# A two-layer decoder step on one core: the second layer's weight loads issued by GpSimd instead of SyncE

## The chip, the core and the metric

The kernel runs on one core of a Trainium2 chip. The core has a matrix engine (TensorE, "PE" in the profile, with its weight loads as "PEld"), a vector engine (VectorE, "DVE"), an activation engine (ScalarE, "ACT"), a general engine (GpSimd, "POOL") and SyncE ("SP"), which does no arithmetic and issues most of the transfers. Each engine takes its instructions strictly in order. A transfer is issued by one engine and carried out by the core's 16 DMA engines. The metric is the device time of one execution in microseconds (us). Lower is better.

## The reference, cut to what matters

One inference step of a two-layer hybrid decoder, for a prompt of 2048 positions and 8 short sample sequences:

```
layer 0:  u = rmsnorm(x); q, k, v, gate, g_low = split(u @ a_w_in)
          o = gated linear attention over chunks (4 heads)
          h = x + (rmsnorm(o) * silu(gate)) @ a_w_out
shared:   k, v = rope(rmsnorm(u @ w_k)), u @ w_v        # once, u = rmsnorm(h)
layer 1:  q, gate = split(rmsnorm(h) @ b_w_in)          # 2048 columns each
          o = attention of q over the last 128 positions and itself, with sinks, 32 heads on 4 key heads
          y = h + (o * silu(gate)) @ b_w_out
```

All is asked in float32. The kernel gets this from float16 products by splitting every factor into a high and a low half and taking three products (`PASSES`).

## The kernel before

The prompt is cut into 16 blocks of 128 positions (`NCH`). Three stages matter here.

**Layer 0 and the preparation.** While layer 0 runs, the weights of layer 1 are prepared beside it. `Unit.prepare` loads a raw float32 piece, scales and splits it (`convert`) and writes the halves to a DRAM tensor `pre`. These writes are issued by GpSimd (`pool.dma_start`, `pre<-pst` in the profile). `form_steps` does the same for the output weights: it forms seven combinations of quarter matrices (`wfd[0]` to `wfd[6]`, `wf<-...`), also written by GpSimd.

**Layer 1, the attention (from about 1420 us).** The loop `for t in range(-3, NKV * NCH)` runs over 64 (group, block) pairs: four groups `g` of 8 heads, 16 blocks in each. An iteration weaves the projections of block `t + 3` (24 matmuls for q, 24 for the gate, 24 more for keys and values in group 0), the scores of block `t + 1` (four steps "A") and the products with the values of block `t` (two steps "B"), by the string `ORDER`. The order of the matmuls is written out by hand (`pin`). For a block:
- `q_norm` squares q on ACT, sums on DVE, takes the power on POOL (`rs_m`, `rs_r`), multiplies on DVE (`KQ<-pj,rs_r`) and rotates on POOL (`KQ<-KQ,bt`, `S<-KQ,bt`, `KQ<-KQ,S`). `q_split` splits (`qe<-KQ`, ACT then DVE) and SyncE transposes by DMA (`X<-qe`, two buffers). `X` is the stationary operand of the scores (`o<-gl,X`, `lev<-gl,X`).
- `scores` takes the softmax numerators; each pair of heads ends in a DMA transpose on SyncE (`sth<-v` and `pst<-v`, two buffers each) that the value products need (`kv<-gl,sth`, `kv<-gl,pst`).
- `last` gates the result; `spill_halves` splits it on ACT and POOL (`ogT`), transposes (`og<-ogT`) and writes it out (`oge<-og`).

So SyncE issues six transposes per block besides the plain transfers.

The weights of a group are 8 units of 512 KB (4 of q, 4 of the gate; 4 more for the shared keys and values in group 0). `Unit.fetch` loads each with one DMA into the ring `W` of 12 buffers (`NW`). A group's fetches are put into the program when block 12 of the group before is reached (`run(gw[g + 1].steps())`); a fetch has to wait until PE has done with the buffer that it overwrites.

**The last stage (from about 2500 us).** y is computed for pairs of blocks with the seven prepared factors `wfd[n]`, seven products for a pair (`Pair`). `wform` loads a factor into four `W` buffers and `wform_big` into one buffer of the ring `uT` (four buffers, until then the normed activations), each in four quarters of 512 KB. They are put into the attention loop at fixed iterations (`n == TOT - 14`, `TOT - 7`, `TOT - 4`) and by a list `trickle` at its end.

Outside a few stretches (`fixed`), a planner that models the engines' times chooses the order of instructions on every engine but PE from the order of the program and from what is ready. `sync` and `pool` are thin wrappers around the engines' issue functions.

Of the kernel before, what the change touches and what calls it, by code (L numbers as in the profile page):

```python
# [75 lines left out]
def _body(tc, nc, cp, sb, ps, dr, i, o):  # L76
# [6 lines left out]
    def T(tag, shape, dt, bufs=None):  # L83
        return sb.tile(shape, dt, tag=tag, name=nm(tag), **({} if bufs is None else {"bufs": bufs}))
# [44 lines left out]
    dve, pool, sync = Queue(nc.vector), Queue(nc.gpsimd), Queue(nc.sync)  # L129
# [27 lines left out]
    wfd = [dr.tile([P, 8, 2, 512], F16, tag=f"wf{n}", name=f"wf{n}") for n in range(7)]  # L157
# [59 lines left out]
    class Unit:  # L217
# [62 lines left out]

        def fetch(self):
            self.t = T("W", [P, 2, 1024], F16, NW)
            sync.dma_start(self.t, self.pre)

        def __call__(self, k, hl, s):
            return self.t.rearrange("p z (k c) -> p z k c", c=self.ncol)[:, hl, k, s]
# [789 lines left out]
    pin[0] = True  # L1076
    us[0].load()
    fetch()
    us[1].load()
    fetch(2)  # L1080
    us[2].load()
    fetch()
    us[3].load()
    fetch(7)
# [689 lines left out]
    def wform_big(n, x, box={}):  # L1774

        if x == 0:
            t = box[n] = T("uT", [P, 8, 2, 512], F16, 4)
            wf[n] = lambda k, hl, s=ALL: t[:, k, hl, s]
        ks = slice(2 * x, 2 * x + 2)
        sync.dma_start(box[n][:, ks], wfd[n][:, ks])  # L1780

    def wform(n, x, ts={}):

        t = ts[n, x] = T("W", [P, 2, 2, 512], F16, NW)
        sync.dma_start(t, wfd[n][:, 2 * x : 2 * x + 2])
        wf[n] = lambda k, hl, s=ALL: ts[n, k // 2][:, k % 2, hl, s]

    quarters = lambda f, n: [lambda x=x: f(n, x) for x in range(4)]
# [147 lines left out]
    for t in range(-3, NKV * NCH):  # L1936
        fill = []
        n = t + 3
# [41 lines left out]
        if n in (TOT - 7, TOT - 4):  # L1980
            run(quarters(wform_big, {TOT - 7: 0, TOT - 4: 2}[n]))
        if n == TOT - 14:
            run(quarters(wform, 3))
        if n == TOT - 1:
            trickle += [lambda x=x: pairs[0].load(x) for x in (3, 2)] + quarters(wform_big, 1)
            summing += pairs[0].sums()
        if n == TOT:
            trickle += quarters(wform, 4) + quarters(wform, 5)
        if n == TOT + 1:
            trickle += quarters(wform_big, 6)  # L1990
# [5 lines left out]
    for p_ in range(NCH // 2):  # L1996
# [8 lines left out]
        if p_ in (3, 4):  # L2005
            n = p_ - 3
# [87 lines left out]
```

## Time and profile before

| | |
|---|---|
| runs | 2772.89, 2778.55, 2779.77 us; median 2778.55 |
| the profiled execution's own time | 2779.74 us |
| its span in the profile | 2778.0 us |
| busy in the span | PE 2705.4, DVE 1699.3, ACT 1388.3, POOL 1135.7 us |
| mean granted TensorE clock | 0.992 |
| bytes moved by DMA | 425.35 MB, of which 385.87 MB by the queue of SyncE (q1), 36.09 MB by GpSimd's (q0) |

The profile's times are measured from the start of the span. A line of a view of groups names the source line (nearly all are helpers' lines, L102 for matmuls and L123 for the rest, so the tiles tell what it is), the engine, the operation and the tiles as out<-in. "SPq" is SyncE issuing. The duration of an issue on SP holds its waits; on POOL it is the time that GpSimd is busy with it.

### The profile page before, as it was taken

The numbers are of one execution on the slowest core, as the hardware profiler recorded it, in microseconds if no ns is written. First come the engines' busy times: TensorE is split into PE (matmuls) and PEld (weight loads), VectorE is DVE, ScalarE is ACT, GpSimd is POOL, SyncE is SP. The second block draws the span as 40 slices with busy tenths as digits, with TensorE's granted clock in tenths as the row PEclk, the third lists the DMA queues.
The fourth block names the chain that finished last, engine by engine and source line by source line (L and its number), as shares of the span: only waits on it lengthen the run. The fifth ranks groups of instructions, "written<-read, shape, count | busy, mean of one in ns | idle before, by whom it ended". The sixth has DMA issues, their size and how long they took to land.

```text
span 2778.0 us, 52040 instructions
## 1 busy us (share of the span) xinstructions
PE 2705.4 (97%) x19378; PEld 1389.7 (50%) x19378; DVE 1699.3 (61%) x3476; ACT 1388.3 (50%) x3235; POOL 1135.7 (41%) x1600
## 2 busy tenths in 40 slices
PE   8999999999999999999999999999999999989999
PEld 5444444544454444445445555555555555544444
DVE  7565656666656664446314656677777777777653
ACT  7664645565556554433213555566666666541110
POOL 4334334333423331136206777576566567530000
PEclk9999999999999999999999999999999999999999
DMA  5543335343534345789766778978978889896431
GB/s 171 129 110 92 99 95 139 105 120 109 144 92 128 112 141 168 223 264 274 218 195 128 135 152 161 216 141 152 201 134 152 192 154 187 162 225 196 148 102 58
DMA packets 800135, 425.35 MB, mean 153 GB/s; under 512 B 636368, under 2 KB 708760, under 8 KB 799848
## 3 DMA queue, kind: packets, MB, share of 16 engines
q1 hardware_dynamic: 786632, 385.87, 59.0%
q0 software_dynamic: 11168, 36.09, 3.6%
q8 instruction: 151, 2.47, 0.4%
q14 instruction: 104, 0.85, 0.1%
q10 hardware_dynamic: 2080, 0.07, 0.0%
HBM read 178.75 MB, written 106.50 MB: 103 GB/s over the span
## 4 chain that ended last, share of the span: by engine, by line
PE 62%; DVE 10%; DMA 9%; ACT 9%; POOL 5%; issue 5%; SPq 0%; ACTq 0%; POOLq 0%; DVEq 0%
PE pj L102 35%; PE tr L102 11%; PE o L102 11%; PE kv L102 3%; DMA pst<-v 2%; ACT o L123 2%; PE lev L102 2%; DVE v L123 2%; POOL KQ L123 1%; ACT v L123 1%; DMA W<-in_state_gla_dram 1%; DVE W L123 1%; ACT L123 1%; DVE o L123 1%; DVE X L123 1%
## 5 line engine op out<-in xcount | busy, mean ns | idle before, releaser
L102 PE MATMUL pj<-W,uT 128*128 128x512 f16 x5088 | 1209.8, 382 | 5.5 <-DVE KQ L123 4.0
L102 PEld LDWEIGHTS <-uT 128*128 128x128 f16 x6976 | 651.0, 98 | 698.7 <-issue 24.5
L102 PE MATMUL tr<-W,uT 128*128 128x512 f16 x1536 | 365.6, 379 | 0.0
L123 POOL TENSOR_TENSOR KQ<-KQ,bt 128x256 f32<-128x256 f32 (+1 forms) x176 | 182.7, 1038 | 261.8 <-DVE X L123 207.8
L102 PEld LDWEIGHTS <-X 128*128 128x128 f16 x2744 | 185.0, 98 | 139.1 <-issue 11.1
L123 ACT ACTIVATE o<-o,mx 128x256 f32<-128x256 f32 (+1 forms) x384 | 168.6, 439 | 168.6 <-DVE mx L123 164.7
L123 POOL TENSOR_SCALAR rs_m<-ss 128x1 f32<-128x1 f32 (+3 forms) x186 | 41.8, 225 | 512.9 <-DVE ss L123 392.6
L123 DVE CUSTOM_DVE_ANT_0 o<-o,madd,nsink 128x256 f32<-128x256 f32 (+1 forms) x384 | 183.8, 479 | 45.4 <-PE o L102 41.1
L123 DVE SCALAR_TENSOR_TENSOR v<-o,v 128x512 f16<-128x512 f32 (+1 forms) x192 | 128.9, 672 | 102.7 <-ACT v L123 99.9
L123 POOL TENSOR_TENSOR rs_r<-rs_m,mhalf 128x1 f32<-128x1 f32 (+3 forms) x182 | 184.5, 1014 | 14.2
L102 PEld LDWEIGHTS <-W 128*128 128x128 f16 x2448 | 125.9, 97 | 86.3 <-issue 1.9
L102 PEld LDWEIGHTS <-v 128*128 128x128 f16 x976 | 95.1, 98 | 115.3 <-issue 2.3
L102 PEld LDWEIGHTS <-sg 128*128 128x128 f16 x800 | 77.6, 98 | 93.4 <-issue 1.2
L123 ACT ACTIVATE X<-KQ 128x512 f16<-128x512 f32 x128 | 84.6, 661 | 75.7 <-PE lev L102 42.6
L123 POOL TENSOR_TENSOR ogT<-og,ogT 128x512 f16<-128x512 f32 x64 | 79.2, 1238 | 102.6 <-ACT ogT L123 102.6
L102 PE MATMUL o<-gl,X 128*128 128x256 f16 (+1 forms) x768 | 114.8, 273 | 4.3 <-DMA X<-qe 2.7
L123 ACT ACTIVATE v<-o 128x512 f16<-128x512 f32 (+1 forms) x192 | 111.2, 579 | 3.5
L123 ACT ACTIVATE lev<-lev,mx 128x256 f32<-128x256 f32 (+1 forms) x128 | 56.5, 441 | 104.8 <-DVE mx L123 102.7
L123 DVE TENSOR_TENSOR X<-KQ,X 128x512 f16<-128x512 f32 x128 | 98.7, 771 | 16.6 <-ACT X L123 15.2
L123 POOL DMA_DIRECT2D pre<-pst x72 | 50.8, 708 | 139.8 <-DVE pst L123 136.5
L123 POOL TENSOR_TENSOR bt<-bt 128x256 f32<-128x256 f32 (+6 forms) x112 | 50.1, 447 | 136.1 <-ACT bt L123 129.2
L102 PE MATMUL pj<-W,v 128*128 128x512 f16 x448 | 103.7, 379 | 0.1
(441 smaller groups left out, 4891.0 us busy)
## 6 DMA issues: line engine op xcount, KB each, us to landing
pre<-pst POOLq DMA_DIRECT2D x72, 256.0 KB, 3.8
W<-pre SPq DMA_DIRECT2D x36, 512.0 KB
ogd<-ogk SPq DMA_DIRECT2D x64, 256.0 KB
wraw<-in_b_w_in_dram SPq DMA_DIRECT2D x64, 256.0 KB
oge<-og SPq DMA_DIRECT2D x64, 256.0 KB
wraw<-in_a_w_in_dram SPq DMA_DIRECT2D x52, 256.0 KB
wraw<-in_a_w_out_dram SPq DMA_DIRECT2D x32, 256.0 KB
X<-in_x_prompt_dram SPq DMA_DIRECT2D x32, 256.0 KB
```

Of the source, the lines that this page charges most:

```text
L102: return order(nc.tensor.matmul(*a, **k))
L123: x = f(*a, **k)
```

## The change

Three issue calls go from SyncE to GpSimd. Sources, destinations, sizes and places in the program stay as they are.

```diff
         def fetch(self):
             self.t = T("W", [P, 2, 1024], F16, NW)
-            sync.dma_start(self.t, self.pre)
+            pool.dma_start(self.t, self.pre)
...
     def wform_big(n, x, box={}):
         if x == 0:
             t = box[n] = T("uT", [P, 8, 2, 512], F16, 4)
             wf[n] = lambda k, hl, s=ALL: t[:, k, hl, s]
         ks = slice(2 * x, 2 * x + 2)
-        sync.dma_start(box[n][:, ks], wfd[n][:, ks])
+        pool.dma_start(box[n][:, ks], wfd[n][:, ks])
...
     def wform(n, x, ts={}):
         t = ts[n, x] = T("W", [P, 2, 2, 512], F16, NW)
-        sync.dma_start(t, wfd[n][:, 2 * x : 2 * x + 2])
+        pool.dma_start(t, wfd[n][:, 2 * x : 2 * x + 2])
         wf[n] = lambda k, hl, s=ALL: ts[n, k // 2][:, k % 2, hl, s]
```

These calls issue 36 loads `W<-pre`, 16 loads `uT<-wf` and 12 loads `W<-wf`, 64 in all, of 512 KB each.

## The prediction

> **What bounds the kernel now.** I read the page first, then the windows of the stages.
>
> ```profile
> PE 2705.4 (97%) x19378; PEld 1389.7 (50%) x19378; DVE 1699.3 (61%) x3476; ACT 1388.3 (50%) x3235; POOL 1135.7 (41%) x1600
> q1 hardware_dynamic: 786632, 385.87, 59.0%
> q0 software_dynamic: 11168, 36.09, 3.6%
> ```
>
> PE is busy for 97% of the span, so a change that leaves the matmuls alone can gain only where PE stands still or runs at a lower clock. The table of windows shows where: busy time (and instructions) of PE, PEld, DVE, ACT and POOL, then the granted clock, the busy share of the DMA engines (packets may overlap, so it can pass 1) and GB/s.
>
> ```profile
> 1420.00:1460.00 40.00, 40.00 (x187) 18.14 (x186) 6.39 (x12) 5.53 (x14) 4.98 (x10) 1.00 0.79 246
> 1460.00:1730.00 270.00, 270.00 (x2037) 144.68 (x2036) 157.28 (x405) 143.12 (x413) 191.87 (x272) 1.00 0.74 142
> 1730.00:1760.00 30.00, 25.95 (x224) 13.41 (x222) 12.97 (x34) 12.70 (x36) 16.07 (x22) 0.89 1.08 287
> 1760.00:1966.00 206.00, 205.00 (x1848) 117.46 (x1846) 153.21 (x404) 133.49 (x405) 132.63 (x164) 1.00 0.81 152
> 1966.00:1994.00 28.00, 25.30 (x252) 14.55 (x251) 20.94 (x51) 17.18 (x53) 16.32 (x24) 1.00 1.04 253
> 1994.00:2194.00 200.00, 199.32 (x1805) 114.19 (x1801) 148.33 (x393) 131.15 (x399) 131.26 (x163) 1.00 0.80 149
> 2194.00:2222.00 28.00, 24.89 (x225) 13.71 (x224) 19.15 (x47) 15.89 (x48) 15.38 (x22) 0.94 1.07 253
> 2325.00:2350.00 25.00, 22.65 (x191) 12.65 (x190) 18.09 (x48) 16.36 (x50) 15.37 (x21) 0.97 1.06 218
> 2386.00:2412.00 26.00, 23.18 (x199) 13.18 (x198) 17.41 (x44) 15.06 (x44) 14.58 (x19) 0.96 1.02 206
> 2436.00:2500.00 64.00, 52.21 (x495) 30.48 (x494) 45.63 (x100) 29.25 (x81) 16.67 (x21) 0.89 0.94 231
> ```
>
> The long quiet stretches lose almost nothing (1.0 us of 206, 0.7 of 200). All the loss of the attention stage sits in six short windows, and these are the windows with the moved loads: three changes of group (1730, 1966, 2194) and three places where factors are fetched (2325, 2386, 2436). There the DMA engines are at 0.94 to 1.08 against 0.80 between. PE's idle time there is 4.05 + 2.70 + 3.11 + 2.35 + 2.82 + 11.79 = 26.8 us. The clock takes more: the share not granted, times the window, is 3.3 + 1.7 + 0.75 + 1.0 + 7.0 = 13.8 us (0.11 of 30, 0.06 of 28, 0.03 of 25, 0.04 of 26, 0.11 of 64). So 40.6 us lie within reach, and hardly more. The view of PE's waits between 1420 and 2510 us (total, times, longest) says on what:
>
> ```profile
> PE kv L102 <- DMA pst<-v: 15.4, 6, 3.5
> PE pj L102 <- DVE KQ L123: 4.0, 1, 4.0
> PE lev L102 <- DVE v L123: 3.3, 1, 3.3
> PE o L102 <- DMA X<-qe: 2.7, 5, 0.7
> ```
>
> Mostly PE waits for transposes that SyncE issues; never for a weight load. One case in order of time, from the timeline:
>
> ```profile
> 2338.34 1.12 SPq L123 DMA_DIRECT2D uT<-wf  x2
> 2339.51 0.45 SPq L123 DMA_DIRECT2D bt<-rtd  x1
> 2340.07 1.78 SPq L123 DMA_TRANSPOSE pst<-v  x1
> 2347.70 0.47 PE L102 MATMUL kv<-gl,pst 128*128 128x64 f16 x10 [2.10 <-DMA pst<-v]
> ```
>
> The transpose stands right behind two 512 KB loads in the queue of SyncE; it is issued by 2341.85 and PE gets it only at 2347.70, 2.10 us late. The change of group at 1730 loses by another path with the same root:
>
> ```profile
> 1747.80 0.60 ACT L123 ACTIVATE E<-pj 128x512 f32<-128x512 f32 x1 [4.13 <-DMA out_cvp_dram<-E]
> 1752.52 1.03 PE L102 MATMUL pj<-W,uT 128*128 128x512 f16 x2 [4.05 <-DVE KQ L123]
> ```
>
> ACT waits 4.13 us for a small output transfer behind weight loads, and the norm after it (sum, POOL's power, `KQ`) holds PE for 4.05 us.
>
> **The change part by part.** It moves 64 issues: 36 `W<-pre`, 16 `uT<-wf`, 12 `W<-wf`. What they take now on SP, and what like transfers take on POOL (ns, smallest/median/largest; then landing):
>
> ```profile
> L123 POOL DMA_DIRECT2D pre<-pst x72: 672/694/792, 421.7 to 1212.8; - x72
> L123 SPq DMA_DIRECT2D W<-pre x36: 319/462/1928, 1420.2 to 2204.7; - x36
> L123 SPq DMA_DIRECT2D uT<-wf x16: 376/434/1243, 2328.2 to 2498.6; - x16
> L123 POOL DMA_DIRECT2D wf<-Sh x14: 542/558/631, 1137.6 to 1337.8; - x14
> L123 SPq DMA_DIRECT2D W<-wf x12: 382/522/928, 2207.7 to 2467.0; - x12
> DMA to landing us min/median/max: 2.3/4.4/7.9
> ```
>
> *Taken from SP.* At the medians 36 x 0.462 + 16 x 0.434 + 12 x 0.522 = 29.8 us of issue time. Only what stands before a late transpose counts. A group change has 8 to 12 fetches, about 4 to 6 us of SP time in 28 us, and the waits for a buffer, which now block SP. The first 12 loads (1420 to 1460) gain nothing: PE is busy for 40.00 of 40.00 us.
>
> *Added to POOL.* 64 x 0.56 to 64 x 0.69, so 36 to 44 us. I take 0.56, since a `wf` write, like a fetch, has one run in each partition on both sides. POOL is busy for 15 to 17 us of each of these windows and has room; but a fetch that waits for its buffer now holds POOL, and behind it stand the rotations of q (`KQ`, `S`), the power, the softmax weights (`dn`, `sg`) and `ogT`, for which DVE, ACT and the transposes wait. How much cover that has, the timeline around the second group change tells:
>
> ```profile
> 1966.87 1.25 SPq L123 DMA_TRANSPOSE sth<-v  x1
> 1968.95 1.28 POOL L123 TENSOR_TENSOR KQ<-KQ,S 128x512 f32<-128x512 f32 x1
> 1970.01 2.40 SPq L123 DMA_DIRECT2D W<-pre  x2
> 1970.92 1.78 DVE L123 TENSOR_TENSOR qe<-KQ,qe 128x512 f16<-128x512 f32 x1 [0.30 <-ACT qe L123]
> 1974.45 2.39 SPq L123 DMA_TRANSPOSE X<-qe  x1
> 1980.24 0.61 PE L102 MATMUL o<-gl,X 128*128 128x256 f16 x4 [0.72 <-DMA X<-qe]
> ```
>
> POOL's last rotation ends at 1970.23, the split on DVE at 1972.70. The issue of `X<-qe` ends at 1976.84 and an issue that waits for nothing takes 1.25, so it was held until 1975.6: for 2.9 us something other than POOL is later. Four fetches in one block cost POOL 4 x 0.56 = 2.2 us, still under that cover. Were it gone, each further 0.56 us would go straight to PE, since `X` arrives exactly when PE needs it (0.72 us late).
>
> *The DMA engines.* The bytes stay. In the first window 246 GB/s take a share of 0.79, so a full set moves 246 / 0.79 = 311 GB/s, and 524,288 B take 1.7 us of all 16 engines. That queue time does not vanish; it can only come earlier. SP now sends the loads late, in between transposes (2338.34 and 2339.07 for quarters whose first half left at 2328); POOL, with its idle time, can send them as buffers come free, before the critical transposes.
>
> *What is won.* Bounds of each place are nothing and its whole loss; without a row for loads in the other queue I take part of the upper end.
> - The factor windows at 2325 and 2386 lose 2.35 + 0.75 and 2.82 + 1.0, together 6.9 us. Without two loads ahead the transpose would come 1.12 us (SP) + 3.4 us (DMA) earlier, more than either stall; if the loads leave at the same moment as before, only the 1.12 us. I take 4.5.
> - The group changes lose 4.05 + 3.3, 2.70 and 3.11 + 1.7, together 14.9 us. I take a third, 5, since engines at 1.04 to 1.08 keep the rest late.
> - The window from 2436 loses 18.8 us. Some of it is the wait on DVE (3.3). Of the rest I take a third, 5.5.
> - Against that, fetches that hold POOL up in blocks with many of them: 4 us, a third of what the second rival below costs.
>
> Sum 4.5 + 5 + 5.5 - 4 = 11 us. The profiled execution took 2779.74 us (span 2778.0 and 1.7 around it), so it would take 2768.7; the median of the runs is 1.2 below it, which gives 2767.5, said as 2768. What is late next at those places is `kv<-gl,pst` still, by less.
>
> **A rule beside it.** The Trainium skill, "DMA: Bandwidth & Descriptors", section "Issuing engines are not separate DMA queues", says that transfers started by several engines run on the same 16 DMA engines and that spreading them saves only the sequencer's time. It speaks against most of this gain and belongs to the first rival; the trace agrees with it as far as the busy shares above 1 go.
>
> **The rivals.**
>
> *The DMA engines decide, not SP (no change).* For: eight loads are 8 x 1.7 = 13.6 us, and 0.81 x 28 = 22.7 us of other work make 36 us of work for a 28 us window, whoever issues it. Against: SP's own order puts loads before late transposes, and the quiet stretches before the windows have a fifth of the DMA time free. Then only SP's 1.12 us at three or four places is won and POOL takes it back: 2777.
>
> *POOL becomes the late one (slower).* A fetch waits on POOL for PE to free its buffer, as two did for SP at 1970.01 (2.40 for two issues of 0.32 at least, so 1.8 us of wait). Four fetches in one block with such a wait are 2.2 + 1.8 = 4.0 us before the last rotation; over the 2.9 us of cover by 1.1 us, and `X` is late by as much in each of some 11 blocks with fetches, 12 us with the stalls of now still there: 2791. It decides from 2.9 us of fetches and waits in one block's chain on POOL. Against it: POOL idles for 12 of 28 us in these windows.
>
> *The other queue goes first (slower).* A packet of q1 has 385.87 MB / 786,632 = 491 B, one of q0 36.09 MB / 11,168 = 3.2 KB. If the engines took a packet from each queue in turn, a load would pass the transposes that were issued before it, which it can't in one queue. One load of 1.7 us more at each of the 6 + 5 waits for transposes is 19 us: 2797. Against it: 256 KB writes by q0 landed after 2.3 to 7.9 us, so q0 itself waits in traffic. This is the rule of the same page's section "Queues, rings and completion order"; by the landing times the trace supports no preference, so it gets a small chance.
>
> **How the numbers follow.** Chances: the forecast 0.48 (2756 to 2771), the DMA engines decide 0.31 (2771 to 2786), POOL late 0.14 (2786 to 2796), q0 first 0.07. About 0.3%, or 8.3 us, is what a measurement of this kernel can tell from no change. Faster by more 0.48, within it 0.32, slower by more 0.20. The low end takes 25 of the 37 us that are left without the wait on DVE, less POOL's 4: 2757. The high end goes into the slower cases until about 1 in 10 is left out: 2790. The planner will also lay out the other engines' instructions anew after 1420, which can move either end by some us.
>
> **What would show it.** Right: q0 has 33.6 MB more; SP has no fetch between transposes; in the windows around the group changes PE's idle time and the lost clock fall; PE's wait for `pst<-v` falls from 15.4 to 9 us or less; the time before 1420 stays. Wrong: `pst<-v` as late as before with DMA shares still above 1 (the DMA engines decide); PE's waits for `X<-qe` above 2.7, with POOL idle on PE before a fetch (POOL late); `sth<-v` and `pst<-v` late also where SP issued them in time (q0 first).

## Result and profile after: 1.7% slower

The changed kernel took 2828.34, 2826.33, 2827.11 and 2819.06 us, median 2826.7; runs of the kernel before beside them had a median of 2778.96 us. The ratio is 1.0166, with a 95% interval of 1.0149 to 1.0184. The profiled execution took 2828.34 us with a span of 2826.5, so 48.5 us are to be found against the span before.

The page after, engines, queues, and the group of PE that waits most:

```profile
PE 2709.1 (96%) x19378; PEld 1390.5 (49%) x19378; DVE 1694.3 (60%) x3476; ACT 1387.9 (49%) x3235; POOL 1170.6 (41%) x1664
q1 hardware_dynamic: 777416, 352.31, 55.1%
q0 software_dynamic: 20384, 69.65, 7.3%
L102 PE MATMUL o<-gl,X 128*128 128x256 f16 (+1 forms) x768 | 114.6, 272 | 33.5 <-DMA X<-qe 30.7
```

PE did the same 19378 matmuls in 3.7 us more (2705.4 before); the other 45 us are idle time. GpSimd has 64 instructions more, and 33.6 MB have gone from q1 to q0 as intended. The transposing `X<-qe`, for which PE waited 2.7 us before, now holds it for 30.7. PE's waits from 1420 to 2555 us (total, times, longest):

```profile
PE o L102 <- DMA X<-qe: 30.7, 10, 13.5
PE kv L102 <- DMA sth<-v: 13.7, 3, 6.7
PE kv L102 <- DMA pst<-v: 6.8, 5, 2.4
PE pj L102 <- DVE sg L123: 6.7, 1, 6.7
```

The wait for `pst<-v` did fall, from 15.4 to 6.8 us; two other transposings took its place, and more. The windows answer to those of before, placed by the same blocks:

```profile
1428.00:1468.00 40.00, 40.00 (x187) 18.13 (x186) 6.40 (x12) 5.60 (x14) 11.54 (x22) 1.00 0.81 212
1739.00:1781.00 42.00, 26.82 (x225) 13.85 (x224) 12.48 (x34) 12.34 (x35) 21.34 (x33) 0.76 0.91 222
1781.00:1990.00 209.00, 206.30 (x1844) 117.54 (x1842) 152.40 (x404) 134.03 (x406) 133.68 (x165) 0.99 0.80 146
1990.00:2023.70 33.70, 26.96 (x252) 15.17 (x250) 19.96 (x52) 17.27 (x54) 21.04 (x32) 0.95 1.01 241
2223.30:2256.60 33.30, 26.06 (x226) 14.24 (x224) 17.83 (x47) 15.72 (x48) 19.81 (x30) 0.85 1.05 243
2468.70:2548.50 79.80, 54.24 (x509) 31.54 (x508) 43.92 (x98) 29.52 (x81) 26.00 (x38) 0.87 0.93 196
```

The three group changes took 30, 28 and 28 us before and take 42, 33.7 and 33.3 now, with as much PE work in each; the last window grew from 64 to 79.8. To sum it without gaps I cut the span at the end of the 24th matmul `tr<-W,uT` of a block, (g, c) being group and block, and give the differences to the span before in us. The other kernels are explained below ("spread, SyncE" is the third version of it, "spread, POOL" the second on GpSimd):

```
                 to     (0,0)   (0,15)  (1,1)   (2,1)   (3,1)   to      end    span
                 (0,0)  ..15    ..(1,1) (2,1)   (3,1)   ..(3,15)(3,15)
                                change  change  change  blocks  on
before         1454.7   279.2    49.0    32.0    33.5   208.3   330.2         2778.0
after            +8.1    +0.7   +15.3    +5.1    +5.3    -2.0   +15.9         +48.6
fetches, POOL    +1.4    +3.7   +13.8    +9.0    +0.4    -2.3    -1.1         +25.2
factors, POOL    +5.9     0.0    -0.6    +0.8   +11.0    -2.3   +22.6         +36.5
POOL's work      +3.4     0.0    +4.2    +3.9    +1.6    -5.1    -1.0          +6.5
ScalarE 4 KB     +1.4    +1.8   +18.4   +11.3    +5.3    -4.3   +18.9         +53.4
ScalarE 1 KB     +9.7     0.0   +12.3    +5.1    +3.1    -2.8    +8.5         +37.1
SyncE 1 KB       +6.2     0.0    -0.4    +1.6    +0.3    -6.1    +1.9          +3.0
spread, SyncE    +5.1     0.0    -1.2    -1.2    -4.2    -5.2    +2.1          -5.0
spread, POOL     +2.5    +3.3    +0.8    +8.2    +5.1    +9.9   +20.2         +50.7
```

The column of a change runs from the last block of the group before to the second of the new one; the stretches between, (1,1) to (1,15) and (2,1) to (2,15), differ by 1.2 us at most and are left out. The first column ends where no moved load has yet had an effect. It is 1.4 to 9.7 us longer in every other kernel, whatever its change, so the profiled execution of before was a short one there; what varies is not settled, and the 8.1 us are not put down to the change.

How a group change stands still, from the timeline after (start, duration, engine; in brackets what ended the wait):

```profile
1742.78 1.59 POOL L123 DMA_DIRECT2D W<-pre  x3
1743.69 5.03 SPq L123 DMA_TRANSPOSE X<-qe  x1
1748.81 10.14 SPq L123 DMA_TRANSPOSE sth<-v  x1
1765.22 1.04 PE L102 MATMUL o<-gl,X 128*128 128x256 f16 x4 [8.45 <-DMA X<-qe]
1767.53 0.54 SPq L123 DMA_DIRECT2D out_cvp_dram<-E  x1
1771.02 0.60 ACT L123 ACTIVATE E<-pj 128x512 f32<-128x512 f32 x1 [15.53 <-DMA out_cvp_dram<-E]
```

`X<-qe` is issued by 1748.72 and lands at 1765.17, 16.5 us later, where some 2 us is usual (a transposing alone, below: 3.1 us less its issue of 1.23). The next transposing holds SyncE for 10.14 us, though an issue takes 1.25; so `out_cvp_dram<-E`, issued at 1743.33 before, leaves at 1767.53, ACT waits 15.53 us to reuse `E`, and PE another 6.7 for `sg`. `qe` was ready at 1741.9 us and `v` at 1748.0, so neither of the two transposings is held for its input. Between the issue of `X<-qe` and its landing q0 moved 4.70 MB, nine loads' worth. Seven of the twelve loads had been issued by 1748.1 and 1.51 MB of them moved, so about four of the nine had been asked for before `X<-qe` and five passed it. Before, SyncE had sent three loads when it came to `X<-qe`. Between 1752 and 1758 us, when both queues had work all the time, the DMA engines did this (packets, MB, time as a share of 16 engines):

```profile
q0 software_dynamic: 529, 1.93, 84.3%
q1 hardware_dynamic: 530, 0.14, 11.8%
```

One packet of q1 for each of q0, and nearly all of the time and bytes to q0: 470 of its packets have 4096 B (median 159 ns each in the packets' records; the other 59 have 4 B), those of a transposing 256 B (18 ns).

### The profile page after: what moved, and what is told of

Its sections match the earlier page's. It is cut to its first block, busy times and chain, and to the rows that moved or that the text cites. A ratio compares the mean times of both kernels' runs of the same rounds, so it can differ in the third digit from the quotient of the medians.

```text
span 2826.5 us, 52042 instructions
## 1 busy us (share of the span) xinstructions
PE 2709.1 (96%) x19378; PEld 1390.5 (49%) x19378; DVE 1694.3 (60%) x3476; ACT 1387.9 (49%) x3235; POOL 1170.6 (41%) x1664
## 4 chain that ended last, share of the span: by engine, by line
PE 59%; DMA 12%; DVE 9%; ACT 9%; issue 6%; POOL 5%; SPq 1%; ACTq 0%; POOLq 0%; DVEq 0%
PE pj L102 33%; PE o L102 11%; PE tr L102 11%; PE kv L102 3%; DMA X<-qe 2%; DMA pst<-v 2%; ACT o L123 2%; DVE v L123 2%; POOL KQ L123 2%; ACT v L123 1%; DMA W<-in_state_gla_dram 1%; SPq L123 1%; PE lev L102 1%; DMA pre<-pst 1%; DVE W L123 1%
## 5 line engine op out<-in xcount | busy, mean ns | idle before, releaser
L123 POOL TENSOR_TENSOR rs_r<-rs_m,mhalf 128x1 f32<-128x1 f32 (+3 forms) x182 | 184.5, 1014 | 13.9
L102 PE MATMUL o<-gl,X 128*128 128x256 f16 (+1 forms) x768 | 114.6, 272 | 33.5 <-DMA X<-qe 30.7
L123 DVE TENSOR_TENSOR X<-KQ,X 128x512 f16<-128x512 f32 x128 | 98.1, 767 | 18.0 <-ACT X L123 16.3
```

The source lines that it names most:

```text
L102: return order(nc.tensor.matmul(*a, **k))
L123: x = f(*a, **k)
```

## Experiments

The theories: **A**, the DMA engines take one packet of each queue in turn. A transposing of 256 KB has 64 packets on each of 16 engines, a load of 512 KB has 8, so a transposing lets up to 8 loads of the other queue pass, 64 x 0.159 = 10.2 us, whichever was issued first. **B**, GpSimd's issues and waits make its other work late. **C**, the loads come at another time or in greater number at once, whatever their packets.

**The disputed wait by itself.** The computation is left out. One transposing on SyncE is released together with twelve loads, four times for each case. (The loads of the other queues in fact begin 1.0 to 1.3 us before the transposing's issue, those on SyncE behind it.)

```
for name, eng, runs in cases:            # tpool: GpSimd, 1 run of 4 KB a partition; tpoolk: 4 of 1 KB; tpoolq: 16 of 256 B
    ...                                  # tact, tactk, tactq: ScalarE; tsp: behind it on SyncE; talone: no loads
    keep(nc.sync.dma_start(out[rep % 2], src, transpose=True))
    if eng is not None:
        for n in range(12):
            load(eng, n, runs, W[n])
```

> The disputed cost by itself; the whole computation is left out. One DMA transpose of 256 KB on SyncE is released together with twelve 512 KB loads, four times each: no loads; loads behind the transpose on SyncE; loads from GpSimd and from ScalarE with runs of 4 KB; the same two with runs of 1 KB and of 256 B. Theory A (the DMA engines take one packet from each queue in turn, so a transpose of 64 packets of 256 B for each engine waits for 64 packets of the loads): alone about 3.2 us from issue to landing; behind-loads on SyncE about 3.2; 4 KB loads from either other engine 64 x 0.18 = 11 us more; 1 KB runs some 3 us more where a run is a packet; 256 B runs about 1 us more. Theory B (GpSimd's own work and waits make the change slow): all cases land about the same, 3 to 5 us. Theory C (only more bytes at the same moment): the landing does not depend on the size of the runs, and ScalarE's loads act as GpSimd's.

Its groups; the last number is VectorE's wait for four transposings:

```profile
L58 DVE CAST stamp<-tact 128x1 f32<-128x1 f16 x4 | 0.6, 154 | 65.5 <-DMA tact<-src 65.5
L58 DVE CAST stamp<-tpool 128x1 f32<-128x1 f16 x4 | 0.6, 154 | 61.6 <-DMA tpool<-src 61.6
L58 DVE CAST stamp<-tpoolk 128x1 f32<-128x1 f16 x4 | 0.6, 154 | 49.7 <-DMA tpoolk<-src 49.7
L58 DVE CAST stamp<-tactk 128x1 f32<-128x1 f16 x4 | 0.6, 154 | 32.1 <-DMA tactk<-src 32.1
L58 DVE CAST stamp<-tpoolq 128x1 f32<-128x1 f16 x4 | 0.6, 154 | 33.1 <-DMA tpoolq<-src 33.1
L58 DVE CAST stamp<-tactq 128x1 f32<-128x1 f16 x4 | 0.6, 154 | 28.2 <-DMA tactq<-src 28.2
L58 DVE CAST stamp<-talone 128x1 f32<-128x1 f16 x4 | 0.6, 153 | 12.5 <-DMA talone<-src 12.5
L58 DVE CAST stamp<-tsp 128x1 f32<-128x1 f16 x4 | 0.6, 154 | 12.4 <-DMA tsp<-src 12.4
```

A transposing alone takes 3.1 us; with the loads behind it in its own queue 3.1; with the same loads in GpSimd's queue 15.4, in ScalarE's 16.4. So it isn't GpSimd. The extra 12.3 and 13.3 us have two parts. The transposing's first packet starts some 4 us after its issue instead of 1.2, as loads that were asked for before it would make it in any order of the queues. From then on the queues take turns. The queues' packets in a stretch inside one transposing, with 4 KB runs on GpSimd (138 to 146 us), with 1 KB runs on ScalarE (309 to 311) and with 256 B runs on GpSimd (655 to 657):

```profile
q0 software_dynamic: 823, 2.98, 92.2%
q1 hardware_dynamic: 824, 0.21, 11.6%
...
q10 hardware_dynamic: 255, 0.26, 55.5%
q1 hardware_dynamic: 877, 0.22, 67.4%
...
q0 software_dynamic: 58, 0.21, 36.0%
q1 hardware_dynamic: 764, 0.20, 86.4%
```

With 4 KB runs it is one for one, as A says, and so in seven of the eight repeats (in the first on GpSimd, 601 for 921); engines that worked in the order of the requests would not alternate.

The shorter runs decide less than they were meant to. On ScalarE's queue runs of 1 KB bring the wait to 8.0 us and of 256 B to 7.0, where A gives 3.1 + 64 x 0.049 = 6.2 and 3.1 + 64 x 0.025 = 4.7 with the recorded times of such packets. But a load then also takes longer to issue (547 to 3429 ns on ScalarE, against 334 to 985), and 255 packets beside 877 are not one for one: its queue often had none to give. On GpSimd the packets stay at 4096 B by the records, whatever the runs, and still 256 B runs bring the wait to 8.3 us; only 58 of them went beside 764. So how many of the other queue's packets are ready counts beside their size. The bytes did not come at the same moments, and C isn't ruled out by these cases. The 12.4 us for 1 KB runs on GpSimd is a mean of 8.4, 11.7, 13.3 and 16.2, with 0, 12, 27 and 31 packets of 4 KB that took over 1.6 us each, ten times the usual.

**The dose.** Three transposings in a row, and 0, 4, 8 or 12 loads; again without the computation.

```
for x in range(3):
    keep(nc.sync.dma_start(out[x], src, transpose=True))
for n in range(many):
    load(eng, n, 1, W[n])
```

> The whole computation is left out. Three transposings of 256 KB in a row on SyncE's queue, released together with no, 4, 8 or 12 loads of 512 KB from GpSimd's queue, from ScalarE's, or 12 behind them on SyncE's own; VectorE waits for the third transposing, four times each. One transposing alone had taken 3.1 us, its 64 packets an engine 18 ns each, so three alone come to about 5.4 to 7. A, packets in turn and nothing else: the third transposing ends after the 192 packets of the three and as many of the loads' as there are, 8 an engine and load at 159 ns: + 5.1 us for 4 loads, + 10.2 for 8, + 15.3 for 12, from either queue, and nothing for 12 on SyncE's own. D, transposings and loads of two queues slow each other's packets beyond taking turns, as between 1983 and 1993 us of the spread kernel on GpSimd, where 29 of 258 packets of 4 KB took over 1.6 us: half as much again or more, 4 loads + 8 us or more.

VectorE's waits, four times each:

```profile
L59 DVE CAST stamp<-xptwelve 128x1 f32<-128x1 f16 x12 | 1.1, 148 | 84.7 <-DMA xptwelve<-src 84.7
L59 DVE CAST stamp<-xpeight 128x1 f32<-128x1 f16 x12 | 1.1, 147 | 67.2 <-DMA xpeight<-src 67.2
L59 DVE CAST stamp<-xatwelve 128x1 f32<-128x1 f16 x12 | 1.1, 147 | 66.4 <-DMA xatwelve<-src 66.4
L59 DVE CAST stamp<-xaeight 128x1 f32<-128x1 f16 x12 | 1.1, 147 | 63.8 <-DMA xaeight<-src 63.8
L59 DVE CAST stamp<-xpfour 128x1 f32<-128x1 f16 x12 | 1.1, 147 | 47.1 <-DMA xpfour<-src 47.1
L59 DVE CAST stamp<-xafour 128x1 f32<-128x1 f16 x12 | 1.1, 147 | 43.5 <-DMA xafour<-src 43.5
L59 DVE CAST stamp<-xstwelve 128x1 f32<-128x1 f16 x12 | 1.1, 147 | 23.8 <-DMA xstwelve<-src 23.8
L59 DVE CAST stamp<-xnone 128x1 f32<-128x1 f16 x12 | 1.1, 147 | 23.7 <-DMA xnone<-src 23.7
```

Above the 5.9 us without loads, GpSimd's cost 5.9, 10.9 and 15.3 us for 4, 8 and 12, where A gives 5.1, 10.2 and 15.3; ScalarE's 5.0 and 10.0 for 4 and 8; twelve on SyncE's own queue cost nothing. ScalarE's twelve cost only 10.7, since no more than nine were there to pass: in the last repeat the first transposing was issued at 450.72 us, nine loads by 458.4, and the last three at 465.8, when that transposing had landed. The dose agrees with A, but doesn't tell it from engines that work in the order of the requests: four or five loads are issued before the first transposing's issue ends, and the loads on SyncE stand behind all three. GpSimd's means for four and eight loads each hold one long repeat, 14.7 us (the others at most 10.8) and 20.7 (15.3 to 15.6), and in these two 12 and 14 packets of 4 KB took over 1.6 us; no other repeat here has more than three. This is theory D of the expectation, and it shows in two of the twelve repeats with GpSimd's loads. The view of the tile in the twelve-load case shows SyncE held as in the kernel: issues last 1.23 us at least and 11.49 at most.

```profile
L55 SPq DMA_TRANSPOSE xptwelve<-src x12: 1232/4328/11491, 162.2 to 244.3; - x12
```

**One half of the change at a time.**

```
-            sync.dma_start(self.t, self.pre)              # fetches alone
+            pool.dma_start(self.t, self.pre)
```
```
-        sync.dma_start(box[n][:, ks], wfd[n][:, ks])      # factors alone
+        pool.dma_start(box[n][:, ks], wfd[n][:, ks])
-        sync.dma_start(t, wfd[n][:, 2 * x : 2 * x + 2])
+        pool.dma_start(t, wfd[n][:, 2 * x : 2 * x + 2])
```

Fetches alone:

> Only the 36 fetches of layer 1's weights are issued by GpSimd, the 28 loads of factors stay on SyncE. The changed kernel loses 15 us at the first change of group, 5 us at the second and 5 at the third: if each place pays for its own loads, 2779 + 25 = about 2804 us, up to 2812 if the 8 us before 1460 us come with it. If the places pull each other (a late start of one makes the next cheaper), less than 2795.

Factors alone:

> Only the 28 loads of factors are issued by GpSimd. In the changed kernel the two early factor windows cost 2 us less than before and the end 16 us more: about 2793 us if each place pays for itself; 2779 or less if the end's loss came from the fetches before.

Fetches alone took 2805.04 us, ratio 1.0098 (1.0070 to 1.0127); factors alone 2812.82, 1.0117 (1.0089 to 1.0145). The fetches came out at the 2804 expected, though not place by place (13.8, 9.0 and 0.4 us where I had 15, 5 and 5); the factors missed their 2793 by 20 us. In the table each loses where its own loads stand: the fetches at the first two group changes, the factors at the third (four factor loads meet it) and at the end. The four fetches of the third change cost nothing by themselves. In ratios the two kernels' losses add to 2.2%, more than the 1.7% of both halves together. At the third change this shows: +11.0 with the four factor loads alone in GpSimd's queue and the fetches on SyncE, +5.3 with both in GpSimd's.

**GpSimd's work without its queue.** Loads stay on SyncE; each waits for a memset of 512 columns by GpSimd.

```
             self.t = T("W", [P, 2, 1024], F16, NW)
+            pool.memset(self.t[:, 0, :512], 0.0)
             sync.dma_start(self.t, self.pre)
```

> All 64 loads stay on SyncE, but each waits for a GpSimd write of 512 columns to its buffer, which takes about as long as the issue did there and waits for the same buffer. So GpSimd gets the work and the waits of the change, and the queue of the loads stays SyncE's. Theory A (turns between the queues): 2775 to 2792 us, transposes are not starved. Theory B (GpSimd late): 2810 us or more.

It took 2787.84 us, 9.8 above the runs beside it, ratio 1.0034 (1.0020 to 1.0048), with 31.6 us of work added to GpSimd (1167.3 busy) where the change adds 34.9. PE's wait for `X<-qe` is 5.9 us. So B exists, at about a fifth of the loss.

**Another queue without GpSimd, and shorter packets in the kernel.** All 64 loads from ScalarE, then the same with `pre` and `wfd` kept in DRAM in runs of 1 KB with a gap behind each, then these runs on SyncE as the control.

```
-            sync.dma_start(self.t, self.pre)
+            nc.scalar.dma_start(self.t, self.pre)                       # 4 KB; the factors alike
```
```
-            self.pre = dr.tile([P, 2, 1024], F16, ...)
+            self.pre = dr.tile([P, 2, 2, 544], F16, ...)                # 1 KB runs; wfd alike
-            sync.dma_start(self.t, self.pre)
+            nc.scalar.dma_start(self.t.rearrange(...), self.pre.rearrange(...)[:, :, :512])    # control: sync
```

> All 64 loads of before (W<-pre, W<-wf, uT<-wf) are requested by ScalarE into its own queue instead of by SyncE; GpSimd does nothing new. A, the engines take one packet of each queue in turn, so that a transposing of 64 packets on an engine waits for about 64 packets of 4 KB: the group changes lose as in the changed kernel (the wait for X<-qe between 1740 and 1770 us some 8 us, + 10 to 15 us for that group change, 5 each for the next two), 2800 to 2830 us. B, GpSimd's own work and order were the cost: not slower than before, 2765 to 2780. C, bytes asked for at another time, whatever the packets: as A, and the same with 1 KB runs (the next kernel).

> As the kernel before it, with the prepared weights and factors kept in DRAM in runs of 1 KB with a gap of 64 B behind each, so that ScalarE's queue has packets of 1024 B instead of 4096 B; the writes to DRAM come in 1 KB runs as well. By the small kernel a transposing beside such loads waits 8.0 us instead of 16.4, with 3.1 alone. A: most of the loss is gone, the group change at 1750 us within 4 us of before, 2775 to 2795 us. B: as the kernel before it. C: as the kernel before it, 2800 to 2830, since bytes and requests are the same.

> Control for the shorter runs: 1 KB runs with gaps, loads on SyncE as in before. All theories: near before, 2770 to 2790 us; what it differs from before is the price of the runs (writes and loads in more packets) and is to be taken off the kernel with 1 KB runs on ScalarE's queue.

They took 2834.61 us, ratio 1.0212 (1.0189 to 1.0236); 2810.02, 1.0121 (1.0105 to 1.0137); and 2788.97, 1.0045 (1.0029 to 1.0062). Queue 10 of the two, with the same bytes in 24576 packets more:

```profile
q10 hardware_dynamic: 11296, 33.63, 4.4%
...
q10 hardware_dynamic: 35872, 33.63, 4.4%
```

ScalarE's queue loses 55.6 us, as much as GpSimd's and more (and just beyond the range expected): B is not the main cause. What ScalarE's own 64 issues and their waits add isn't separated. Against its control the 1 KB kernel loses 21.0 us, against 55.6: C, for which packets don't matter, would have added the control's 10 us instead. An issue of a load takes ScalarE 0.53 us there at the median instead of 0.33, far less of a difference than in the small kernel. But my expectation of 2775 to 2795 was missed. The group change at 1750 us lost 12.3 us where I expected 4. PE's longest wait for `X<-qe`, at that change, fell from 17.8 to 5.8 us, as A says (in all, PE still waits 25.8 us for it, after 40.8), but `out_cvp_dram<-E` in the same queue came late all the same, and ACT behind it (timeline of the 1 KB kernel):

```profile
1763.42 1.04 PE L102 MATMUL o<-gl,X 128*128 128x256 f16 x4 [5.84 <-DMA X<-qe]
1769.26 0.60 ACT L123 ACTIVATE E<-pj 128x512 f32<-128x512 f32 x1 [10.54 <-DMA out_cvp_dram<-E]
```

By A each of SyncE's transfers in a row pays for its own packets, which one transposing by itself doesn't show; that this is all of the 12.3 us is argued.

**Fewer loads at once.** A load is tied to a block by a tiny copy into its buffer, so that the planner can't draw it forward; four units of groups 2 and 3 and the quarters of three factors come one a block. A group change then has 8, 4 and 4 loads instead of 12, 8 and 8 (the counts in two of the expectations are wrong in this).

```
-        def fetch(self):
+        def fetch(self, after=None):
             self.t = T("W", [P, 2, 1024], F16, NW)
+            if after is not None:
+                dve.tensor_copy(self.t[:1, 0, :1], after)          # after = blk.sg[:1, :1]
...
+        if n < NKV * NCH and c in (2, 4, 6, 8) and g in (1, 2):
+            gw[g + 1].q.units[c // 2 - 1].fetch(blk.sg[:1, :1])
```

> Candidate that keeps all loads on SyncE, behind the transposes of their own queue, and spreads those that aren't urgent: the four q units of groups 2 and 3 and the quarters of factors 0, 2 and 3 each behind a one-element VectorE copy that reads the current block's sg, one or two blocks apart; a group change then has 12, 8 and 4 loads at once changed to 12, 8 or 4 fewer where the q units went ahead (eight units at change 0 to 1 and 1 to 2 stay, the q units come earlier). A: waits at the later group changes and in the windows from 2325 us shrink, 2760 to 2776 us. B and C have nothing against a like gain, from fewer loads in one burst. If the waits there were not set by the burst, within 5 us of before.

2775.84 us, ratio 0.9988 (0.9977 to 0.9998). The changes gained 3.0, 3.5 and 5.0 us, and blocks (1,10), (2,10) and (3,6) lost 3.7, 4.3 and 4.6. The second version put three of the loads elsewhere:

> The spread loads on SyncE of the kernel before, with two places changed: the fourth q unit of groups 2 and 3 is asked for with block 5 instead of 8, and the second and third quarters of factor 3 with 13 and 12 blocks to go instead of 12 and 10. There the blocks (1,10), (2,10) and (3,6) had taken 17.6, 18.7 and 19.0 us, against 13.9, 14.4 and 14.4 before. A: a load that lies directly ahead of an X<-qe in SyncE's queue costs its 1.4 us of engine time and what SyncE is held, and elsewhere nothing; so these three blocks come back to within 1 us of before, and the kernel takes 2758 to 2770 us. If the places don't matter: 2770 to 2778, with other blocks longer.

2776.54 us, 0.9999 (0.9986 to 1.0012): missed. (1,10) and (2,10) were back at 13.9 and 14.5, but (2,7) took 15.6 instead of 13.5 and (3,6) stayed at 19.5. I put (3,6) down to the copy of the third quarter, at 2286 us, as if VectorE had stood there for a buffer that PE still used. The trace doesn't bear that out: VectorE was idle for 0.03 us before that copy, and for no more than 0.04 before any of the twenty. `X<-qe` came late there, 4.5 us for PE, and why stays open. The third:

> The spread loads on SyncE with the places of three of them changed again: q units with blocks 2, 3, 4 and 6 (block 5's load stood ahead of an X<-qe at 2079 us, block (2,7) 15.6 us against 13.5), and the third quarter of factor 3 with 9 blocks to go instead of 12, where its buffer came free only at 2286 us, behind which VectorE stood in block (3,6) (19.5 us against 14.4 before). (2,7) and (3,6) come back to within 1 us of before: 2764 to 2774 us. If (3,6) stays at 19, its cause is another and the kernel is the same as before.

2775.34 us, 0.9986 (0.9976 to 0.9997). (2,7) is back at 13.5, (3,6) at 16.3, 1.9 above before, not within 1, and (3,5) took 15.6 instead of 13.5. Its windows at the last two group changes and the two factor windows:

```profile
1971.00:1999.00 28.00, 25.95 (x269) 14.90 (x268) 21.44 (x53) 18.02 (x56) 17.20 (x24) 1.00 1.03 227
2199.00:2227.00 28.00, 27.32 (x269) 15.48 (x266) 22.17 (x56) 17.71 (x52) 17.19 (x23) 1.00 1.05 226
2325.00:2350.00 25.00, 24.92 (x228) 14.17 (x226) 19.59 (x56) 17.62 (x54) 15.67 (x22) 1.00 0.97 190
2386.00:2412.00 26.00, 26.00 (x221) 14.84 (x219) 19.91 (x53) 16.07 (x48) 15.30 (x20) 1.00 0.95 200
```

PE is idle there for 2.05, 0.68, 0.08 and 0.00 us, against 2.70, 3.11, 2.35 and 2.82 before. In the last two windows this need not be the spread's doing: with the same loads unspread on SyncE in 1 KB runs, the blocks (3,1) to (3,15) are 6.1 us shorter than before, with GpSimd's added work 5.1, here 5.2. At the group changes all three versions gain, 1.2 to 5.0 us each, where those two kernels lie between -0.4 and +4.2. This version beats the changed kernel by 1.8% and the one before by 0.14%, with an interval that ends just short of no change and after three tries; a gain over before is likely, not shown. It leaves the queue as it was.

The second version with its 64 loads on GpSimd:

> The same spread, with all 64 loads requested by GpSimd as in the changed kernel: 12, 4 and 4 loads at the group changes instead of 12, 8 and 8, the factors of the window from 2325 us one a block. A, loss only where many loads stand beside transposes at once: change 0 to 1 loses its 12 to 15 us as in the changed kernel (12 loads), 1 to 2 and 2 to 3 at most 3 us each against the spread on SyncE, the end some 10 to 16 us: 2785 to 2805 us. B, GpSimd's work for each load: each of the three group changes loses about as in the changed kernel or more by the added waits, 2810 to 2830.

2818.71 us, ratio 1.0145 (1.0120 to 1.0170), which fits neither A's 2785 to 2805 nor, in the places, B. The first change, now with 8 loads, lost 0.8 us instead of 15.3. But the second, with 4, lost 8.2, where I had allowed 3, and the end 20.2. So the number of loads doesn't set the loss: eight cost 0.8 us here and 5.1, 9.0 and 11.3 at the second change of the changed kernel, the fetches alone and ScalarE; four cost 8.2 here, 0.4 at the third change of the fetches alone and 11.0 there with the factors alone. Packets taking turns can't make the 8.2: in the second change `X<-qe`, issued by 1981.6, landed at 1996.6 while only three loads passed. The DMA engines were slow in themselves there, 138 GB/s from 1983 to 1993 us against 345 in the changed kernel from 1752 to 1758:

```profile
DMA packets 1453, 1.38 MB, mean 138 GB/s; under 512 B 1062, under 2 KB 1195, under 8 KB 1453
```

Of the 258 packets of 4 KB in it 29 took over 1.6 us. The ScalarE kernel has such a stretch too (121 GB/s from 1752 to 1764 us). Such packets come with the second queue. Of the loads' 8192 packets of 4 KB, over 1.6 us in the attention and its end (1420 to 2560 us) were: 1 before and 1 to 7 in the three spread kernels on SyncE, but 67 in the changed kernel, 49 and 54 with one half of the change, 128 here and 168 with ScalarE. The small kernels have them too, as told above. What makes these packets slow stays open.

## Why the prediction was wrong

I forecast 2768 us, and it took 2826.7, outside the range.

**The step that failed is the one that put aside the third rival, "the other queue goes first".** It rested on a mean over the whole program, 491 B a packet of q1, and on landing times of 2.3 to 7.9 us, which are those of q0's `wf` writes at 1137 to 1338 us. Both hid the attention. Q1 of the kernel before, over those writes and over a quiet stretch of attention:

```profile
q1 hardware_dynamic: 32818, 34.90, 61.5%
...
q1 hardware_dynamic: 131057, 37.87, 73.7%
```

That is 1063 B a packet there and 289 B here. The larger the packets on the other side, the fairer are turns; beside the 256 B of a transposing they gave q0 84.3% of the time and q1 11.8%. The Trainium skill's rule ("DMA: Bandwidth & Descriptors", section "Queues, rings and completion order"), that an engine goes from queue to queue with a whole packet each, was the right one, and the measured 529 and 530 packets bear it out, one for one; how many of them the engine takes at a turn, no run shows.

**The rival's price was mis-sized too.** It let one load of 1.7 us pass at each wait, 19 us in all. A transposing lets as many packets pass as it has itself, 64 an engine, so up to 8 loads, 10.2 us; with loads that were asked for before it, and that GpSimd asks for sooner than SyncE did, 12.3 us in the small kernel and 14.5 at 1748.7 us (16.5 less the 2 of a transposing alone). And it comes again in each transfer behind it, and in the small outputs that SyncE can't issue meanwhile.

**Point by point.**
- *Bytes and queues*: right, q0 has 33.6 MB more, SyncE no fetch between transposings. The first 12 loads: right, PE was busy for 40.00 of 40.00 us again.
- *Transposings behind weight loads in SyncE's queue were the loss*: in part. Spreading the loads gains 1.2 to 4.2 us at each of the three group changes in its third version, with the queue unchanged. But that SyncE's queue kept the transposings from being passed by later loads was worth more, and I hadn't counted it. In the small kernel twelve loads behind a transposing in one queue cost it 0 us.
- *Factor windows, 4.5 us won*: the blocks (3,1) to (3,15) gained 2.0, but 2.3 with the factors left on SyncE, and 5.1 and 6.1 in two kernels with all loads there. So this isn't shown to be the change's doing; a new layout by the planner would do it, which is argued, not shown.
- *Group changes 5 us and last window 5.5 us won*: they lost 25.7 and 15.9.
- *GpSimd's term, 4 us*: 9.8 us by the kernel with its work alone; the second rival's 12 us was nearer, and still not the cause.
- *The reach of 40.6 us*: the sum holds. Its 13.8 us of clock not granted are no idle time counted twice: from 1420 us on in the kernel before the clock stood at half in seven stretches of 3.4 or 6.8 us after PE's waits, 30.7 us together, and PE was busy for 27.6 of them (at 1753 us a matmul of 512 columns every 0.43 us, at 1762 every 0.22). What failed was the way to reach it. After, the clock at the first change fell from 0.89 to 0.76, while PE's busy time rose by only 0.9 us (25.95 to 26.82), so there most of the lost clock does lie in idle time.
- *What would show it*: `pst<-v` at 9 us or less was to be the sign that I was right. It came (6.8), with `X<-qe` eleven times as long. A sign that looks at one of three transfers of the same kind is not one.
- "DMA: Bandwidth & Descriptors" of the Trainium skill, section "Issuing engines are not separate DMA queues", which I had taken to mean no change, held in that the engines are shared. It says that only the sequencer's time is saved; here the move cost 1.7%.

Of the 48.5 us 39.6 lie at the group changes and the end, less the gain in the blocks between (15.3 + 5.1 + 5.3 + 15.9 - 2.0), and A with B and the slow packets account for their kind. How each place divides between turns, loads asked for sooner, slow packets and waits on GpSimd is not settled, nor are the 8.1 us before them.

## What to carry to other kernels

Before a transfer is moved to another queue, ask what its old queue kept in order: bulk loads behind small urgent transfers let these go first, in a queue of their own they take a packet for each of theirs. Reckon with packets in the stretch concerned, not bytes, and not a mean over the program: the small transfer's packets on one engine times the time of the other queue's packet is a first estimate of the wait that it can get (10.2 us here, measured 12.3 and 13.3). Where bursts of loads are in the way of urgent transfers, try spreading the loads before changing their queue; here that was worth 0.1%, if anything, and the other queue cost 1.7%.

## What the runs showed of the hardware

- With two queues at work, 529 packets of one went with 530 of the other, at 4096 and 256 B nearly all, and 823 with 824 in the small kernel. Where the other queue's packets weren't ready it was fewer (58 with 764). Each 512 KB load of GpSimd's queue added about 1.3 us to three transposings released with it (15.3 us for 12).
- GpSimd's queue moved packets of 4096 B whether runs were 4096, 1024 or 256 B; ScalarE's and SyncE's made a packet of each run (24576 packets more for 1 KB runs in both).
- SyncE is held in the issue while its queue's packets wait: up to 11.49 us for an issue of 1.23, and what stands behind it, wanted or not, isn't issued.
- In two kernels with a second queue the DMA engines moved 121 and 138 GB/s for 12 and 10 us at a busy share of 1.16. Packets of 4 KB over 1.6 us, where 159 ns is the median, number 49 to 168 in the kernels with 4 KB loads in a second queue and 1 to 7 with them on SyncE. Not explained.
